# The low-half score pass of a head over 128 rows instead of 64, with zeros in a tile per head

## Chip, core and metric

The kernel runs on one core of a Trainium2 chip (trn2). The metric is the device time of one execution in microseconds (us); of several runs the median counts. Matrix products run on TensorE (PE; its weight loads stand in the trace as PEld), elementwise work on VectorE (DVE), ScalarE (ACT) and GpSimd (POOL), transfers are issued from the queue of SyncE (SP) or of POOL.

## What is computed

A sequence of 512 tokens with 1024 features goes through a block with three mixing branches and a feed-forward part, and then through two layers, each with eight heads of softmax attention ("fox" in the code), eight heads of retention ("ret") and a gated feed-forward part. The change touches the score products of three kinds of heads, 64 features wide: those of the first branch, of fox and of ret. Cut from the reference:

```
s = jnp.einsum('bqhd,bkhd->bhqk', q_blk, k_band).astype(jnp.float32) * scale + bias
...
logits = jnp.einsum('bhqd,bhkd->bhqk', qb, k).astype(jnp.float32) * scale
logits = logits + cq[..., :, None] - cum[..., None, :]
...
scores = jnp.einsum('bhid,bhjd->bhij', qc, kc) * intra_decay
```

## The kernel before

All activations lie feature-major: 128 features on the partitions, 512 tokens along the row. Every fp32 matrix is cut into two exact halves of the type fp32r (`xh`, `xl` of an activation, `wh`, `wl` of a weight), and a linear layer is three matmuls of 128x128 weights by 512 columns for each block of 128 features (`lin`, names `lin<-xh,wh`, `lin<-xh,wl`, `lin<-xl,wh`). These fill most of PE's time. The halves of the weights are made while the kernel runs, `wh` by ACT and `wl` by DVE.

Two heads of 64 features lie in one 128-row tile of q and one of k. `stack` (line 802) makes from such a pair: `ks`, a tile per head with the high half of k in the head's own 64 rows and the low half in the other 64; `qd`, a tile per head with the high half of q twice; and `ql`, one tile for both heads with the low half of q, each head in its own rows. A block of scores is then two products in one PSUM bank: `qd` with `ks` over 128 rows, and `ql` with `ks` over the head's 64 rows only:

```
return [[(qd[e], ks[e]), (ql[64 * e:64 * e + 64], ks[e][64 * e:64 * e + 64])] for e in range(2)], ...
```

`head` (line 825, first branch and fox) emits for each head four blocks of 128 queries with 128, 256, 384 and 512 keys; fox adds a third product with the constants `mkb` in bf16 that masks the diagonal block. `ret` (line 1713) emits four blocks of 128 keys with 512, 384, 256 and 128 queries. Every block is followed by DVE work that frees the PSUM bank (`lg<-sc,E`, or `st<-sc,dec`), then ACT, DVE and POOL, transposes (`pt`) and the products with the values (`po`).

The order is set when the program is recorded: every part is a coroutine, `Net.drive` (line 301) takes the ready one of the highest priority, and "ready" follows an estimated time of PE (`mm`, line 378) and of the queues of DVE, ACT and POOL (`Eng`, line 211). Each engine then runs its instructions in that fixed order. Tiles of 128x512 come from one pool of 66 (`g`), in the same order. DVE, ACT and POOL work is recorded by one helper (line 221), all matmuls by line 379, transposes by line 389.

Of the kernel before, what the change touches and what calls it, by code (L numbers as in the profile page):

```python
# [87 lines left out]
def _fm(w, kc=8):  # L88
    """[K, M] -> [M/128, K/(128*kc), 128, kc*128]: lhsT tiles, one column block at a time."""
    k, m = w.shape  # L90
    return np.ascontiguousarray(
        w.reshape(k // (128 * kc), kc, 128, m // 128, 128).transpose(3, 0, 2, 1, 4)
    ).reshape(m // 128, k // (128 * kc), 128, kc * 128)


def _tok(w):
    """[1024, 512] -> [4, 128, 2*512]: rhs rows, two row blocks per chunk."""
    return np.ascontiguousarray(w.reshape(4, 2, 128, 512).transpose(0, 2, 1, 3)).reshape(4, 128, 1024)


def _nar(w):
    """[1024, m] -> [128, 8*m]: lhsT rows of a narrow block."""
    return np.ascontiguousarray(w.reshape(KT, 128, -1).transpose(1, 0, 2)).reshape(128, -1)
# [98 lines left out]
class Ev:  # L202
    """a point in PE time, known once the work before it has been traced."""
# [7 lines left out]
class Eng:  # L211
    """an engine's instructions, with an estimate of when its queue is done."""
# [35 lines left out]
class Net:  # L248
# [39 lines left out]
    def w(self, *engs):  # L288
        """ns until the queues of these engines are done and seen to be."""
        return max(0.0, max(self.busy[e] for e in engs) - self.now) + self.LAT  # L290
# [4 lines left out]
    # ------------------------------------------------- cooperative emission  # L295
    # Each coroutine traces instructions and yields where a later one would wait:
    # None (go on at once), ns of PE time, an Ev, or a predicate.
# [46 lines left out]
    def take(self, role, n, cap):  # L344
        """wait for a place among the cap of a role."""
        while self.role.get(role, 0) + n > cap:
            yield lambda: self.role.get(role, 0) + n <= cap
        self.role[role] = self.role.get(role, 0) + n
# [43 lines left out]
    # ---------------------------------------------------------------- basics  # L392
# [32 lines left out]
    # ------------------------------------------------------ weights, linear  # L425
# [43 lines left out]
    def nextw(self):  # L469
        """the next chunk of weights as exact halves; the ones after it are set going."""  # L470
        i, n = self.wi, len(self.wq)
        if self.booting:
            self.wi += 1
            return self.wh.pop(i), self.wl.pop(i)
        self.fill()
        while self.wsh < min(n, i + 4):
            self.whi()
            while self.wsl < min(self.wsh - 1, i + 3):
                self.wlo()
        while self.wsl < min(n, i + 3, self.wsh):  # L480
            self.wlo()
        self.wi += 1
        return self.wh.pop(i), self.wl.pop(i)
# [19 lines left out]
    def lin(self, ps, w, off, xs, start=True, stop=True):  # L503
        """accumulate W^T x, each product of halves in its own pass."""
        wh, wl = w
        for k, x in enumerate(xs):
            yield from self.need(x)
            c = slice(off + 128 * k, off + 128 * k + 128)
            first, last = start and k == 0, stop and k == len(xs) - 1
            self.mm(ps, wh[:, c], x.h, first, False)  # L510
            self.mm(ps, wl[:, c], x.h, False, False)
            self.mm(ps, wh[:, c], x.l, False, last)
            yield None

    def proj(self, chunks, xs, evac):
        """task: one 128-row block of outputs; chunks: (dram, cols); xs: thunk."""
# [14 lines left out]
    def narrow(self, w, m, xs, evac):  # L531
        """task: a block of m outputs; the halves of its weights stand side by side, rows m to 2 m add to the first m."""
# [16 lines left out]
    def group(self, w, cut, xs, evacs):  # L549
        """task: several blocks at once, their last k tile after all the others; w: dram [blocks, 128, cols]."""  # L550
# [19 lines left out]
    def multi(self, chunk, parts):  # L570
        """task: one chunk that holds several blocks; parts: (offset, xs thunk, evac)."""
# [25 lines left out]
    def split(self, src, X_, free=True):  # L597
        """src -> hi, lo entries (coroutine)."""
# [10 lines left out]
    # ------------------------------------------------------------------ norm  # L609
    def feed(self, N, k, x, gain, done=None):  # L610
        """tile k of a norm's input: g x as halves, and its squares."""
# [34 lines left out]
    def rowsum(self, ps, a, n):  # L646
        """(coroutine) sums over each n rows of a feature-major tile, token-major: [128, S / n]."""
# [8 lines left out]
    def powm(self, src, n, scale, eps):  # L656
        """(coroutine) (scale src + eps)^-1/2."""
# [9 lines left out]
    def bcast(self, rt, n=NT):  # L667
        """(coroutine) token-major [128, NT] -> [128, S], the same on all partitions."""
# [11 lines left out]
    def rstd(self, N, n=D, eps=EPS):  # L680
        """(coroutine) 1/rms: N.rt token-major, N.rb broadcast."""
# [17 lines left out]
    # ------------------------------------------------------------- attention  # L699
    def values(self, chunks, nks, N, vs, centred=False):  # L700
        """task: token-major values, split: vs[t][e] = [keys, pair, (hi, lo) or (lo, hi), 64]."""
# [75 lines left out]
    def pv(self, h, vs, ph, pl, evs, y, yev):  # L777
        """(coroutine) y[rows of head h] = values^T p."""
# [23 lines left out]
    def stack(self, q, k):  # L802
        """(coroutine) a pair's q and k as exact halves, for two passes of products per head:
        [qh; qh] with [kh; kl], then ql with kh. Head 1 has its kh in the lower rows."""
        qh = yield from self.g("qh", F32R)
        self.ac.activation(qh, q.h, AF.Copy)
        qd, ks = [], []
        for e in range(2):
            r = slice(64 * e, 64 * e + 64)
            ks.append((yield from self.g("ks", F32R)))  # L810
            self.ac.activation(ks[e][r], k.h[r], AF.Copy)
        yield self.w("ac")
        ql = yield from self.g("ql", F32R)
# [6 lines left out]
        self.dv.tensor_tensor(out=ql, in0=q.h, in1=qh.bitcast(F32), op=ALU.subtract)  # L820
        self.free(qh, q.h, k.h)
        yield self.w("dv", "gp", "ac")
        return [[(qd[e], ks[e]), (ql[64 * e:64 * e + 64], ks[e][64 * e:64 * e + 64])] for e in range(2)], [[qd[0], ks[0]], [qd[1], ks[1], ql]]

    def head(self, h, qk, vs, y, yev, bias, mask, qdone, hdone):
        """(coroutine) softmax attention; q carries -scale, so scores come negated."""
# [70 lines left out]
    # --------------------------------------------------------------- block 1  # L897
# [73 lines left out]
    def load_x(self, N):  # L971
        """(coroutine) x and the first weights, in the order in which the first products take them."""
# [56 lines left out]
    def qk(self, w, N, out, c=None):  # L1029
        """task: projection to an fp32 tile (entry out)."""  # L1030
        self.proj([(w, 1024)], lambda: N.xs, self.qkev(N, out, c))
# [11 lines left out]
    def after(self, vs, n):  # L1043
        """count the heads that are done with vs."""
        vs.left -= n
        if vs.left == 0:
            self.vfree(vs)

    def heads(self, pr, q, k, vs, y, mk, mask, prio=2):
        """(coroutine) the two heads of a pair -> y entry. q, k: entries per head, rows of a head."""  # L1050
# [67 lines left out]
    def gates(self, n, upto, N):  # L1118
        """tasks: the gates of branch n below `upto` that are not yet there."""
# [61 lines left out]
    # ------------------------------------------------------------ HGRN branch  # L1181
    def logsig(self, z, f, s, out):
        """(coroutine) log sigmoid(z), with f = sigmoid(z) and s = sigmoid(-z); f is overwritten."""
# [10 lines left out]
    def gnorm(self, o, eps):  # L1194
        """(coroutine) per-head mean square of a pair tile -> 1/sqrt(ms + eps), broadcast in PSUM."""
# [24 lines left out]
    def silu(self, z):  # L1220
        """(coroutine) z <- z sigmoid(z)"""
# [7 lines left out]
    def blocks(self, t, off, stride, n, w):  # L1229
        """n blocks of w columns, `stride` apart, of a flat tile."""  # L1230
# [113 lines left out]
    def hlev(self, q, k, pre, suf, fifo):  # L1344
        """(coroutine) per level: q exp(sum since the block's middle), k exp(sum up to it)."""
# [35 lines left out]
    def near(self, t, n, dg):  # L1381
        """(coroutine) scores with at most one per key: the products t, at their keys, summed over each head."""
# [10 lines left out]
    def level(self, qt, kt, n, dg):  # L1393
        """(coroutine) scores of one level on the diagonal blocks, kept where they belong."""
# [54 lines left out]
    # ------------------------------------------------------------------- FFN  # L1449
    def xadd(self, m, ps, nxt=None):  # L1450
        """(coroutine) residual add of block m, then what follows it."""
# [46 lines left out]
    # --------------------------------------------------------------- block 2  # L1498
    def fin1(self, N1, N, m):
        """closing norm of block 1 folded with the opening norm of layer 0."""  # L1500
# [123 lines left out]
    def xout(self, m):  # L1624
        """block m of the residual stream to DRAM while attention needs the room."""
# [21 lines left out]
    def fgate(self, i, ps, N, cum):  # L1647
        """(coroutine) running sum of log sigmoid(f + bias), to DRAM for the broadcast loads."""
# [40 lines left out]
    def rotary(self, w, N, out, c, rot):  # L1689
        """task: projection with the rotary embedding."""  # L1690
# [85 lines left out]
    def ple_proj(self, i, half, out):  # L1776
        """tasks: half of p @ w_ple_proj, kept for the gate."""
# [132 lines left out]
    def last(self, chunks, N, pp, N4):  # L1910
        """task: the last two blocks of the gate in two halves of the tokens, each with its share of the closing norm."""
# [74 lines left out]
class BranchC:  # L1986
    """latent attention: shared preparation, then its pairs of heads."""
# [32 lines left out]
    def tables(self):  # L2020
        """cos and signed sin of position * frequency, 16 frequencies per 32 rows."""
# [143 lines left out]
class X:  # L2165
    """a tile (h), or its exact halves (h, l), ready at ev; s: the rows that count."""
# [40 lines left out]
```

## Time and profile before

| | |
|---|---|
| median of 3 runs | 2363.28 us (2362.02 to 2363.62) |
| profiled execution, first to last instruction | 2362.3 us |
| PE busy | 2326.2 us, 98% |
| DVE busy | 1509.7 us, 64% |
| ACT busy | 1070.2 us, 45% |
| POOL busy | 455.0 us, 19% |

The span of the profiled execution lies 1.0 us under the median of the runs. The recorded end of a matmul is modelled and overlaps the next one, so that PE counts as busy even where its matmuls start far apart; the distance from start to start is what a matmul costs.

### The profile page before, as it was taken

To read this page: it belongs to the slowest core of one execution; us is meant where nothing else is said; L and a number is where in the kernel's file an instruction comes from. 1 tells how busy PE (TensorE), PEld (TensorE's weight loads), DVE (VectorE), ACT (ScalarE), POOL (GpSimd) and SP (SyncE) were. 2 spreads that over 40 slices of the span, in tenths; PEclk is the share of its full clock that TensorE was granted. 3 is DMA by queue.
4 is the path that set the end of the run, shared out by engine and by line. 5 is a ranking of instruction groups with operands and counts; after the bars stand their busy time and mean duration, and the time that the engine had idled before them with its cause. 6 is when DMAs were issued, how large, how long until landed. Compare 5 with 4: busy or idle time off the path is not lost.

```text
span 2362.3 us, 28970 instructions
## 1 busy us (share of the span) xinstructions
PE 2326.2 (98%) x10810; PEld 1871.6 (79%) x10810; DVE 1509.7 (64%) x2355; ACT 1070.2 (45%) x1695; POOL 455.0 (19%) x531
## 2 busy tenths in 40 slices
PE   9999999999999999999999999999999999999998
PEld 7787877778888888777778888888777778888887
DVE  6778489976542554678866562457578866552466
ACT  5657466664321233555543331245555544331343
POOL 3423044431000002323330000002323320000012
PEclk9999999999999999999999999999999999999999
DMA  5222222223322332432332333333332332333332
GB/s 181 75 68 63 81 72 63 63 85 116 98 95 98 98 98 83 152 95 89 117 98 94 98 98 98 104 93 115 123 104 81 107 107 90 98 98 98 107 91 70
DMA packets 75725, 228.23 MB, mean 97 GB/s; under 512 B 9664, under 2 KB 15680, under 8 KB 75584
## 3 DMA queue, kind: packets, MB, share of 16 engines
q1 hardware_dynamic: 70400, 209.62, 28.2%
q0 software_dynamic: 5184, 16.75, 2.3%
q8 instruction: 85, 1.39, 0.3%
q14 instruction: 56, 0.46, 0.1%
HBM read 215.29 MB, written 6.32 MB: 94 GB/s over the span
## 4 chain that ended last, share of the span: by engine, by line
PE 91%; DVE 6%; issue 1%; ACT 1%; POOL 1%; DMA 0%; SPq 0%; POOLq 0%; DVEq 0%; ACTq 0%
PE lin L379 75%; PE v L379 6%; PE sc L379 5%; PE po L379 3%; PE pt L389 1%; DVE wl L221 1%; DVE dg L221 1%; DVE xl L221 1%; DVE eq L221 1%; DVE pre L221 0%; DVE suf L221 0%; DVE sl L221 0%; DVE gate L221 0%; ACT L221 0%; PE pb L389 0%
## 5 line engine op out<-in xcount | busy, mean ns | idle before, releaser
L379 PE MATMUL lin<-xh,wh 128*128 128x512 f32 (+1 forms) x2752 | 1095.9, 398 | 0.0
L379 PE MATMUL lin<-xl,wh 128*128 128x512 f32 (+1 forms) x2752 | 1072.4, 390 | 6.7 <-DVE xl L221 6.6
L379 PE MATMUL lin<-xh,wl 128*128 128x512 f32 (+1 forms) x2728 | 1061.8, 389 | 0.0
L221 DVE TENSOR_TENSOR wl<-raw,wh 128x1024 fp32r<-128x1024 f32 (+3 forms) x391 | 467.6, 1196 | 513.4 <-PE lin L379 335.7
L221 ACT ACTIVATE wh<-raw 128x1024 fp32r<-128x1024 f32 (+4 forms) x394 | 392.5, 996 | 821.7 <-PE lin L379 684.9
L379 PEld LDWEIGHTS lin<-xl,wh 128*128 128x128 f32 x2752 | 517.3, 188 | 117.7 <-DVE xl L221 8.8
L379 PEld LDWEIGHTS lin<-xh,wh 128*128 128x128 f32 x2752 | 517.4, 188 | 117.0 <-issue 11.7
L379 PEld LDWEIGHTS lin<-xh,wl 128*128 128x128 f32 x2728 | 514.2, 188 | 96.1
L221 POOL TENSOR_TENSOR sq<-sq 128x512 f32<-128x512 f32 (+1 forms) x61 | 90.6, 1485 | 571.5 <-ACT sq L221 570.8
L221 POOL TENSOR_SCALAR P<-P,r 128x128 f32<-128x128 f32 (+3 forms) x128 | 80.3, 633 | 198.7 <-DVE r L221 180.8
L221 POOL MEMSET pad<- 128x2 f32 x44 | 4.4, 100 | 586.7 <-DVE cv L221 586.7
L221 DVE SCALAR_TENSOR_TENSOR cv<-pad,vec,cv 128x512 f32<-128x512 f32 x88 | 66.1, 752 | 40.7 <-ACT cv L221 39.0
L221 DVE CUSTOM_DVE_ANT_0 lg<-sc,E 128x128 f32<-128x128 f32 (+1 forms) x96 | 46.6, 486 | 60.9 <-PE sc L379 53.7
L379 PE MATMUL v<-wh,xh 128*128 128x512 f32 x192 | 78.2, 407 | 2.3 <-POOL wh L221 2.3
L379 PE MATMUL v<-wl,xh 128*128 128x512 f32 x192 | 75.6, 394 | 1.5 <-DVE wl L221 1.4
L221 ACT ACTIVATE ph<-pt 128x512 fp32r<-128x512 f32 (+3 forms) x128 | 55.7, 435 | 45.5 <-PE pt L389 44.5
L379 PE MATMUL v<-wh,xl 128*128 128x512 f32 x192 | 75.5, 393 | 0.0
L221 ACT ACTIVATE P<-lg,m 128x128 f32<-128x128 f32 (+1 forms) x96 | 53.5, 558 | 39.7 <-DVE m L221 28.9
L221 DVE TENSOR_TENSOR x<-lin,x 128x512 f32<-128x512 f32 x80 | 54.6, 684 | 23.5 <-PE lin L379 23.4
L221 DVE TENSOR_TENSOR pl<-pt,ph 128x512 fp32r<-128x512 f32 (+3 forms) x128 | 60.4, 481 | 13.8 <-ACT ph L221 13.3
L221 ACT ACT_TABLE_LOAD x51 | 65.4, 1283 | 4.3 <-DVE qk L221 1.6
L221 ACT ACTIVATE tl<-po 64x512 f32<-64x512 f32 x56 | 33.2, 593 | 74.0 <-PE po L379 73.6
(243 smaller groups left out, 2558.6 us busy)
## 6 DMA issues: line engine op xcount, KB each, us to landing
raw<-wup SPq DMA_DIRECT2D x88, 512.0 KB, 3.3
raw<-w SPq DMA_DIRECT2D x83, 512.0 KB, 3.6
raw<-wf SPq DMA_DIRECT2D x64, 512.0 KB, 3.3
raw<-wdn SPq DMA_DIRECT2D x32, 512.0 KB, 3.5
raw<-wv SPq DMA_DIRECT2D x22, 512.0 KB, 3.6
raw<-wpg SPq DMA_DIRECT2D x16, 512.0 KB, 3.3
raw<-wbr SPq DMA_DIRECT2D x12, 512.0 KB, 3.3
raw<-wdn SPq DMA_DIRECT2D x16, 384.0 KB, 3.1
```

Of the source, the lines that this page charges most:

```text
L221: r = f(*a, **k)
L379: self.nc.tensor.matmul(out, l, r, start=start, stop=stop)
L389: self.nc.tensor.transpose(out, src, self.ident)
```

## The change

`stack` now makes a `ql` tile for each head: DVE writes the low half of q to the head's own 64 rows (two instructions of 64 rows in place of one of 128), POOL writes zeros to the other 64. The second product runs `ql` with the whole `ks` over 128 rows; the zeros take the low half of k out of the sum. A `ql` tile is freed with its own head. The rest of the diff takes out comments and docstrings and is not shown.

```diff
-        qd, ks = [], []
+        qd, ks, ql = [], [], []
         for e in range(2):
-            r = slice(64 * e, 64 * e + 64)
+            r, o = slice(64 * e, 64 * e + 64), slice(64 - 64 * e, 128 - 64 * e)
             ks.append((yield from self.g("ks", F32R)))
             self.ac.activation(ks[e][r], k.h[r], AF.Copy)
+            ql.append((yield from self.g("ql", F32R)))
+            self.pl.memset(ql[e][o].bitcast(F32), 0.0)
         yield self.w("ac")
-        ql = yield from self.g("ql", F32R)
         for e in range(2):
...
-        self.dv.tensor_tensor(out=ql, in0=q.h, in1=qh.bitcast(F32), op=ALU.subtract)
+        for e in range(2):
+            r = slice(64 * e, 64 * e + 64)
+            self.dv.tensor_tensor(out=ql[e][r], in0=q.h[r], in1=qh[r].bitcast(F32), op=ALU.subtract)
         self.free(qh, q.h, k.h)
         yield self.w("dv", "gp", "ac")
-        return [[(qd[e], ks[e]), (ql[64 * e:64 * e + 64], ks[e][64 * e:64 * e + 64])] for e in range(2)], [[qd[0], ks[0]], [qd[1], ks[1], ql]]
+        return [[(qd[e], ks[e]), (ql[e], ks[e])] for e in range(2)], [[qd[0], ks[0], ql[0]], [qd[1], ks[1], ql[1]]]
```

`stack` runs 20 times (4 pairs of the first branch, 4 of fox and 4 of ret in each of two layers).

On DVE this is the first `stack` of the program, as a piece of the difference:

```order
 L221 CAST lev<-lv 128x512
 L221 TENSOR_TENSOR ks<-qk,ks 64x512 x2
-L221 TENSOR_TENSOR ql<-qk,qh 128x512
+L221 TENSOR_TENSOR ql<-qk,qh 64x512 x2
 L221 TENSOR_TENSOR wl<-raw,wh 128x1024
 L221 SCALAR_TENSOR_TENSOR qk<-lin,rb 128x512
```

One instruction has become two at the same place, and the low half of a weight (`wl`) stands behind them.

On POOL this is the same place and the next pair, after the change (before, the two `MEMSET ql` rows are not there):

```order
L221 MEMSET ql 64x512 x2
L221 TENSOR_SCALAR qd<-qh 64x512 x2
L221 DMA E<-ext 128x512
L221 TENSOR_SCALAR E<-E 128x512
L221 MEMSET E 64x64
L221 DMA E<-ext 128x512
L221 MEMSET ql 64x512 x2
L221 TENSOR_SCALAR qd<-qh 64x512 x2
```

The zeros stand ahead of the copies of `qd` and of the load of a head's bias `E`.

The new estimates also shift the order a little. On PE, in the first layer, the second head of the third ret pair and the first head of the fourth stand together before the change:

```order
L379 MATMUL sc<-qd,ks 128x384
L379 MATMUL sc<-ql,ks 128x384
L379 MATMUL lin<-xh,wh 128x512
L379 MATMUL lin<-xh,wl 128x512
L379 MATMUL lin<-xl,wh 128x512
L379 MATMUL sc<-qd,ks 128x256
L379 MATMUL sc<-ql,ks 128x256
L379 MATMUL sc<-qd,ks 128x512
L379 MATMUL sc<-ql,ks 128x512
L379 MATMUL sc<-qd,ks 128x128
L379 MATMUL sc<-ql,ks 128x128
```

and after it the second head of the third pair stands alone, each block of scores followed by a linear step:

```order
L379 MATMUL sc<-qd,ks 128x384
L379 MATMUL sc<-ql,ks 128x384
L379 MATMUL lin<-xh,wh 128x512
L379 MATMUL lin<-xh,wl 128x512
L379 MATMUL lin<-xl,wh 128x512
L379 MATMUL sc<-qd,ks 128x256
L379 MATMUL sc<-ql,ks 128x256
L379 MATMUL lin<-xh,wh 128x512
L379 MATMUL lin<-xh,wl 128x512
L379 MATMUL lin<-xl,wh 128x512
L379 MATMUL sc<-qd,ks 128x128
L379 MATMUL sc<-ql,ks 128x128
```

The first head of the fourth pair has moved some 30 matmuls of linear layers down. Elsewhere the moves are of the same kind; the number of matmuls is unchanged.

## Rows read from the trace of the kernel before

**Rows 1.** The page, busy time: us busy, share of the span, instructions.

```profile
span 2362.3 us, 28970 instructions
...
PE 2326.2 (98%) x10810; PEld 1871.6 (79%) x10810; DVE 1509.7 (64%) x2355; ACT 1070.2 (45%) x1695; POOL 455.0 (19%) x531
```

**Rows 2.** All instructions on the tile ql: count, duration ns min/median/max, first and last start.

```profile
L379 PE MATMUL sc<-ks,ql x96: 322/410/503, 56.9 to 1828.6; 64*128 64x128 f32 x24, 64*128 64x256 f32 x24, 64*128 64x384 f32 x24, 64*128 64x512 f32 x24
...
L379 PE MATMUL sc<-ql,ks x64: 322/408/500, 1065.3 to 1883.7; 64*128 64x512 f32 x16, 64*128 64x384 f32 x16, 64*128 64x256 f32 x16, 64*128 64x128 f32 x16
L221 DVE TENSOR_TENSOR ql<-qk,qh x12: 691/692/1009, 48.8 to 1806.8; 128x512 fp32r<-128x512 f32 x12
```

**Rows 3.** Timeline, first head of the first branch: start us, duration us, engine, instruction.

```profile
56.73 0.22 PE L379 MATMUL sc<-ks,qd 128*128 128x128 f32 x1
...
57.47 0.40 PE L379 MATMUL lin<-xh,wl 128*128 128x512 f32 x1
...
57.94 0.28 PE L379 MATMUL sc<-ks,qd 128*128 128x256 f32 x1
...
58.80 0.39 PE L379 MATMUL lin<-xh,wl 128*128 128x512 f32 x1
...
60.48 0.39 PE L379 MATMUL lin<-xl,wh 128*128 128x512 f32 x1
...
60.70 0.40 PE L379 MATMUL sc<-ks,qd 128*128 128x512 f32 x1
...
61.03 0.18 PEld L379 LDWEIGHTS sc<-ks,ql 64*128 64x128 f32 x1 [0.36 <-issue]
61.03 0.50 PE L379 MATMUL sc<-ks,ql 64*128 64x512 f32 x1
...
61.46 0.50 PE L379 MATMUL lin<-xh,wh 128*128 128x512 f32 x1
...
61.80 0.40 PE L379 MATMUL lin<-xh,wl 128*128 128x512 f32 x1
```

**Rows 4.** Timeline of PE in the first layer: products with values, then a fox head.

```profile
1112.71 0.33 PE L379 MATMUL po<-pl,vs 128*128 128x384 f32 x1
1112.88 0.28 PE L379 MATMUL po<-ph,vs 128*128 128x256 f32 x1
1113.00 0.28 PE L379 MATMUL po<-pl,vs 128*128 128x256 f32 x1
...
1117.04 0.34 PE L379 MATMUL sc<-ks,qd 128*128 128x384 f32 x1
...
1117.68 0.23 PE L379 MATMUL sc<-mkb 128*128 128x128 bf16 x1
```

**Rows 5.** Timeline of the third branch: scores over 96 rows, then the mask.

```profile
177.89 0.38 PE L379 MATMUL sc<-q,q 96*128 96x128 f32 x2
...
178.11 0.22 PE L379 MATMUL sc<-mkb 128*128 128x128 bf16 x1
```

**Rows 6.** Busy time in stretches of the layers, all instructions: us, counts, then PE's granted clock.

```profile
1060.00:1170.00 110.00, 109.67 (x499) 80.30 (x499) 94.02 (x185) 66.72 (x132) 44.55 (x50) 1.00 0.30 89
1140.00:1170.00 30.00, 29.67 (x126) 21.29 (x125) 29.20 (x44) 19.91 (x35) 11.85 (x12) 1.00 0.28 82
```

**Rows 7.** The same stretches, instructions on ql alone: PE, PEld, DVE.

```profile
1060.00:1170.00 110.00, 17.67 (x43) 7.86 (x43) 4.15 (x6) 1.00 0.30 89
1140.00:1170.00 30.00, 4.59 (x11) 2.01 (x11) 1.38 (x2) 1.00 0.28 82
1840.00:1870.00 30.00, 4.58 (x11) 2.01 (x11) 1.39 (x2) 1.00 0.27 87
```

**Rows 8.** DVE on the tile ks, in the form of rows 2.

```profile
L221 DVE TENSOR_TENSOR ks<-ra,ks x16: 684/687/1815, 1061.5 to 1864.0; 64x512 fp32r<-64x512 f32 x16
```

**Rows 9.** POOL's groups: count, busy us, mean ns, idle before and its cause.

```profile
L221 POOL TENSOR_SCALAR qd<-qh 64x512 fp32r<-64x512 f32 x40 | 33.1, 828 | 34.7 <-ACT qh L221 33.0
...
L221 POOL MEMSET dg<- 128x512 f32 x8 | 3.9, 524 | 0.0
```

## Prediction

> **What bounds the kernel now.** I read the page first. PE is busy 98% of the span, DVE 64%, POOL 19% [rows 1], and in the stretches of the layers PE's clock is granted in full (1.00) [rows 6]: the time is what PE's matmuls cost, one after the other. PE's busy time can't tell what one costs, since ends are modelled; the distance from start to start in a timeline can. So I went to the timeline of the first head whose scores are made in the first branch, where all four widths come with linear steps between them.
>
> There the reader sees the normal step first: a linear matmul of 512 columns starts at 60.48 and the next matmul at 60.70, 0.22 us later (0.225 below; the same step is seen for whole linear layers). Then the pattern breaks [rows 3]. `qd` with `ks` starts at 60.70, `ql` with `ks` at 61.03 (0.33 instead of 0.225), the next linear matmul at 61.46 (0.43), and the one after it at 61.80 (0.34). The row of PEld at 61.03 gives the reason: the load of the weights for the 64-row product starts at the moment of its matmul, after 0.36 us in which no load ran, and nothing that the profile shows was waited for. The loads of the products over 128 rows run beside the matmul before. So a product over 64 rows between products over 128 costs 1.10 us for three matmuls that normally take 3 x 0.225 = 0.68: 0.42 us are lost.
>
> Is it the 64 rows, or just a score product? Scores of the third branch run over 96 rows, and there two passes of 128 columns and the start of the mask fit into 0.22 us (177.89 to 178.11), 0.11 each, with no gap [rows 5]. Products with the values over 128 rows follow each other at 0.17 (384 columns, 1112.71 to 1112.88) and 0.12 us (256 columns, 1112.88 to 1113.00) [rows 4]. Only the 64-row forms stand apart. There are 96 + 64 = 160 of them, a quarter at each width [rows 2].
>
> **What the change takes away.** After it both score products are 128-row products like their neighbours, so I price them at the normal steps: 0.225, 0.17, 0.12 and 0.11 us for 512, 384, 256 and 128 columns. The zeros add no columns. From the start of `qd` to the second linear matmul, [rows 3] have 1.10 us at 512 columns (normal 0.68), 0.86 at 256 (normal 0.12 + 0.12 + 0.225 = 0.465) and 0.74 at 128 (normal 0.445). Lost: 0.42, 0.395 and 0.295; 384 columns I put between the two widest, 0.40. The mean is 0.378. The first branch (32 products) and ret (64) are of this kind: 96 x 0.378 = 36.2 us.
>
> In fox the mask in bf16 follows `ql`. Up to its start [rows 4] show 1117.04 to 1117.68, 0.64 us at 384 columns, where 2 x 0.17 = 0.34 are normal: 0.30 lost. What comes behind the mask looks the same in the third branch, where no 64-row product precedes it, so I count nothing there. At the other widths I take the loss above without its last part (0.34 - 0.225 = 0.115): 0.305, 0.28 and 0.18. Mean 0.267, times 64 products: 17.1 us. Together PE has 53.3 us less to do, 0.33 a product.
>
> The Trainium skill (TensorEngine Tiling (Array Packing), Key Properties) says that a change of tiling mode, not of the tile alone, drains the engine. The gaps on both sides of each 64-row product agree with it, and by it the whole 53.3 us would go.
>
> **What it adds.** DVE: one more instruction in each of 20 `stack` calls. The old one over 128 rows took 0.69 us (up to 1.01) [rows 2]; one of the same kind over 64 rows, for `ks`, takes 0.69 as well [rows 8]. So 20 x 0.69 = 13.8 us. Behind it wait `wl` of the coming weights and the work on the scores. POOL: 40 memsets of 64x512; one of 128x512 takes 0.524 us [rows 9], so at most 21 us in all on an engine that is 81% idle. Two of them (1.05 us) stand ahead of the `qd` copies; those idle for ACT's `qh` before they start, 33.0 us over 40 [rows 9], so that about half of the memsets is covered. If this cover is gone, a `stack` comes 1.05 us later, at worst 21 us over all 20, if PE had nothing recorded between; it has linear layers there. One more tile of 128x512 is held per pair: no cost of its own, it shifts the recorded order.
>
> **How much of the 53.3 us arrives.** PE gets ahead only where the others keep up. In 1060 to 1170 of the first layer DVE is busy 94.0 of 110 us, and in its last 30 us 29.2 of 30 [rows 6]. 43 of the layer's 64 products lie in the longer stretch, 11 in the last 30 us, and again 11 in the twin of these in the second layer [rows 7]. Where DVE has no idle time PE can't gain: 22 x 0.33 = 7.3 us don't come. Of the new DVE work, 6 of each layer's `stack` calls fall into the longer stretch (6 old `ql` instructions there, [rows 7]); I charge these in full, 12 x 0.69 = 8.3 us, and hide the rest behind DVE's idle time elsewhere. The bounds of this term are 0 (everything hidden) and 13.8 to 20.2 us (all 20 at 0.69 or 1.01). The order helps a little: the two ret heads that stand together before the change, at the end of the full stretch, stand apart after it; I give it nothing.
>
> Sum: -53.3 + 7.3 + 8.3 = -37.7 us. Against the profiled execution's 2362.3 this is 2324.6; its span lies 1.0 under the median of the runs, so I predict **2325.5 us**.
>
> **The rivals.**
>
> *DVE becomes the bound of the layers.* After the change the stretch of 110 us would hold 110 - 43 x 0.33 = 95.7 us of PE and 94.0 + 6 x 0.69 = 98.1 us of DVE. DVE was packed to 97% in the last 30 us and to 85% over all 110 [rows 6]. At 97% the stretch takes 101.1 us, a gain of 8.9 instead of 14.3; at 93%, 105.5; at 88%, 111.5, a loss of 1.5. In the last case the change gives 53.3 - 2 x 15.8 = 21.7 us: 2341.6. For it speaks that DVE, ACT and PE hand each other the tiles of a head in turn; against it that weight halves are made chunks ahead, so that DVE may lag for a while. Chance 0.20.
>
> *Nothing goes.* The gap could belong to the `ql` product itself, to its operands or to the order in which PE's loads are issued, and stay with 128 rows. Then PE gains nothing and the layers pay the 8.3 us of DVE at most: 2363.3 to 2371.6. The Trainium skill (TensorE: Matmul & The Clock Gate, Part 3: Packing small matmuls) states that a weight load overlaps matmuls in flight only when its row group differs, which speaks against whole-array products: by it the loads of the new passes would lie bare too. Against this the trace has the steps of 0.225 us in which loads over 128 rows run beside matmuls over the same 128 rows [rows 3]; the 96-row scores say the same [rows 5]. Chance 0.07.
>
> *Slower: a memset holds POOL's queue.* A `ql` tile is taken from the pool of 66 earlier than before, and its memset waits for the last reader of the buffer. POOL is in order: behind it stand `qd`, the load of `E` and the scaling of the probabilities, for which PE waits. If each of the 20 calls held PE for 3 us, this would cost 60 us against 53.3 and, with the 8.3 us of DVE, end at 2363.3 + 15 = 2378. It decides from (53.3 - 8.3) / 20 = 2.25 us a call on. Against it stands POOL's idle time, and that a buffer comes back only once the program's estimate has its reader done. Chance 0.06.
>
> *All of it arrives*, 2310 or less, if DVE's new work hides and the full stretches loosen: the lower end of the main case and a little beyond, 0.05 beyond.
>
> **How the numbers follow.** The main case has the remaining 0.62; its own range goes from 2310.0 (nothing charged) to 2337.5 (all of 20.2 us of DVE, and 7.3 that don't come). The range for 8 in 10 reaches into the rival in which DVE bounds the layers and leaves out the two in which nothing is gained: **2307 to 2347 us**. A difference of 0.2% (4.7 us) is about what a measurement here can tell from none. Faster by more: main, DVE and full arrival, 0.62 + 0.20 + 0.05 = 0.87. Within 0.2%: most of the case in which nothing goes, 0.05. Slower: the rest of it and the held queue, 0.08.
>
> **What would show it.** In the changed trace every second score product should read 128x128, its weight load should run beside the matmul before, and `qd`, `ql` and two linear matmuls of 512 columns should start 0.22 to 0.23 us apart. The stretch of each layer's heads should be 14 to 20 us shorter, the first branch about 12, nothing else. DVE should have 20 more instructions and be full for longer near the end of the layers' heads, with some waits of PE for `pl` or `ql` there. I am wrong in the step on the 64 rows if the gap of 0.33 to 0.43 us is still there with 128; wrong in the step on DVE if PE's waits on DVE stay near zero or eat more than 16 us; wrong on POOL if PE or ACT wait for a memset.

## The result and the profile after

The changed kernel takes 2324.09 us (median of 4 runs, 2323.04 to 2325.01), the kernel before 2363.45 us (median of 4 runs, 2362.02 to 2365.72). The ratio is 0.9832, 95% interval 0.9818 to 0.9846: 39.4 us or 1.7% faster. 2325.5 was predicted, with 2307 to 2347 as its range.

The page of the changed kernel, from its first line, its busy times (as in [rows 1]) and its chain of work that ended last:

```profile
span 2323.2 us, 29048 instructions
...
PE 2278.9 (98%) x10810; PEld 1868.2 (80%) x10810; DVE 1518.4 (65%) x2375; ACT 1067.4 (46%) x1695; POOL 479.0 (21%) x571
...
PE 87%; DVE 8%; issue 2%; POOL 1%; ACT 1%; DMA 0%; SPq 0%; POOLq 0%; DVEq 0%; ACTq 0%
```

The kernel is still bound by PE, which issues as many matmuls as before. DVE has its 20 instructions more, POOL its 40. In the chain PE's share is 87% where it was 91%, and DVE's 8% where it was 6%.

Instructions on the tile `ql`, as in [rows 2]:

```profile
L379 PEld LDWEIGHTS sc<-ks,ql x96: 187/188/192, 58.7 to 1793.5; 128*128 128x128 f32 x96
L379 PE MATMUL sc<-ks,ql x96: 273/308/397, 58.8 to 1793.7; 128*128 128x128 f32 x24, 128*128 128x256 f32 x24, 128*128 128x384 f32 x24, 128*128 128x512 f32 x24
...
L221 POOL MEMSET ql<- x40: 517/520/526, 35.1 to 1823.2; 64x512 f32 x40
L221 DVE TENSOR_TENSOR ql<-qk,qh x24: 682/689/1011, 50.1 to 1777.7; 64x512 fp32r<-64x512 f32 x24
L221 DVE TENSOR_TENSOR ql<-ra,qh x16: 682/687/990, 1049.3 to 1832.7; 64x512 fp32r<-64x512 f32 x16
```

The product now reads 128 rows and its recorded time has fallen from 410 ns (median) to 308. The new DVE instructions take the 0.69 us that were charged, a memset of 64 rows takes 0.52.

The timeline of the first heads of the first branch, to be held against [rows 3] (some rows of other engines and of PEld are left out):

```profile
59.64 0.28 PE L379 MATMUL sc<-ks,qd 128*128 128x256 f32 x1
59.75 0.28 PE L379 MATMUL sc<-ks,ql 128*128 128x256 f32 x1
59.87 0.40 PE L379 MATMUL lin<-xh,wh 128*128 128x512 f32 x1
60.10 0.40 PE L379 MATMUL lin<-xh,wl 128*128 128x512 f32 x1
...
61.62 0.39 PE L379 MATMUL sc<-ks,qd 128*128 128x512 f32 x1
61.62 0.19 PEld L379 LDWEIGHTS sc<-ks,ql 128*128 128x128 f32 x1
61.84 0.39 PE L379 MATMUL sc<-ks,ql 128*128 128x512 f32 x1
61.84 0.19 PEld L379 LDWEIGHTS lin<-xh,wh 128*128 128x128 f32 x1
62.07 0.40 PE L379 MATMUL lin<-xh,wh 128*128 128x512 f32 x1
62.31 0.39 PE L379 MATMUL lin<-xh,wl 128*128 128x512 f32 x1
```

At 512 columns the way from `qd` to the second linear matmul is 62.31 - 61.62 = 0.69 us; it was 1.10. At 256 columns it is 0.46, where it was 0.86. The weight load of `ql` now starts at 61.62, together with the matmul before its own.

A fox head of the first layer, to be held against [rows 4]:

```profile
1060.95 0.34 PE L379 MATMUL sc<-ks,qd 128*128 128x384 f32 x1
1061.13 0.34 PE L379 MATMUL sc<-ks,ql 128*128 128x384 f32 x1
1061.31 0.23 PE L379 MATMUL sc<-mkb 128*128 128x128 bf16 x1
```

From `qd` to the mask it is 0.36 us; it was 0.64.

The loss at all 160 products can be added up: for each the steps from start to start of the matmul before it, of its own and of the one behind, less the normal step of their width (0.227, 0.174, 0.119 and 0.110 us for 512, 384, 256 and 128 columns). That makes 51.4 us before (13.0 in the first branch, 38.4 in the two layers) and 1.4 us after; these 1.4 are two waits for `pl`, 0.7 us each, that fall among the steps counted. So PE has 50.0 us less to do, and 39.4 arrive. A good part of the rest shows as waits that are new or longer. The view of PE's waits of the changed kernel has among others, by cause (us in total, times, longest):

```profile
PE pt L389 <- POOL P L221: 3.9, 6, 1.3
PE po L379 <- DVE pl L221: 2.4, 4, 0.7
```

Before, PE never waited for `P`, and for `pl` once, 0.2 us. Waits for `wl` and `eq` also grew, by 1.7 and 1.1 us, and one for `wh` shrank by 1.6. Windows of the stretch of the layers' heads, the first layer and then the second (length, then busy us of PE, PEld, DVE, ACT, POOL, PE's granted clock, and at the end the DMA's share and GB/s):

```profile
1040.00:1150.00 110.00, 106.42 (x543) 87.23 (x543) 100.77 (x197) 68.36 (x134) 56.74 (x67) 1.00 0.32 99
1730.00:1840.00 110.00, 106.21 (x538) 87.19 (x537) 99.83 (x201) 69.08 (x137) 52.63 (x61) 0.98 0.32 101
```

DVE is busy for 100.8 of 110 us there; in the like stretch before it was 94.0 [rows 6]. The timeline shows how a wait for `P` comes about (first layer; rows of several views, the others left out; an entry in brackets is the idle time before the instruction and what ended it):

```profile
1065.98 0.15 DVE L221 RECIPROCAL r<-sum 128x1 f32<-128x1 f32 x1
1066.16 4.64 POOL L221 TENSOR_SCALAR P<-P,r 128x256 f32<-128x256 f32 x1
1066.37 0.68 DVE L221 TENSOR_TENSOR rb<-rb,rot 128x512 f32<-128x512 f32 x1
1066.97 0.15 DVE L221 RECIPROCAL r<-sum 128x1 f32<-128x1 f32 x1
...
1068.43 0.54 DVE L221 TENSOR_TENSOR pl<-st,ph 128x384 fp32r<-128x384 f32 x1
1068.90 1.21 DVE L221 TENSOR_TENSOR wl<-raw,wh 128x1024 fp32r<-128x1024 f32 x1
1070.04 0.41 DVE L221 TENSOR_TENSOR pl<-st,ph 128x256 fp32r<-128x256 f32 x1
...
1070.85 0.33 PE L389 MATMUL pt<-cst,P 128*128 128x128 f32 x1 [1.33 <-POOL P L221]
1071.44 0.33 PE L389 MATMUL pt<-cst,P 128*128 128x128 f32 x1 [0.26 <-POOL P L221]
1072.14 0.33 PE L389 MATMUL pt<-cst,P 128*128 128x128 f32 x1 [0.37 <-POOL P L221]
```

POOL scales the probabilities `P` by reciprocals `r`, which DVE makes. The reciprocals are not late: the last of this head's is done at 1067.12. It is POOL's own instruction that is long: one on a `P` of 128x256 lasts 4.64 us, where the median of its shape is 0.48 and the longest before the change was 1.83. All that time DVE runs without a gap (rotary products, `st`, `pl`, halves of weights), and POOL's instruction ends 0.35 us after a subtraction for `pl`. PE's transposes wait behind it. The second layer has the same, 4.64 us from 1751.19. That DVE's work holds POOL's instruction is inferred from these times; rot_out, below, bears on it.

In the second layer the clock falls behind this wait (a window as above):

```profile
1757.00:1760.40 3.40, 3.23 (x10) 2.78 (x11) 0.76 (x2) 1.18 (x3) 2.22 (x5) 0.50 0.77 264
```

PE has waited for `P` for 1.30 and 0.26 us, and from 1757.0 on its clock is granted at half (0.50), that is 1.2 GHz, for 3.4 us; the matmuls that start there take some 1.5 us more than their normal steps. This is where the 0.98 above comes from. The kernel before has no such stretch between 1243 and 1939. What is left of the 10.6 us that did not arrive is not assigned to causes here.

### The profile page after: what moved, and what is told of

Its sections match the earlier page's. It is cut to its first block, busy times and chain, and to the rows that moved or that the text cites. A ratio compares the mean times of both kernels' runs of the same rounds, so it can differ in the third digit from the quotient of the medians.

```text
span 2323.2 us, 29048 instructions
## 1 busy us (share of the span) xinstructions
PE 2278.9 (98%) x10810; PEld 1868.2 (80%) x10810; DVE 1518.4 (65%) x2375; ACT 1067.4 (46%) x1695; POOL 479.0 (21%) x571
## 4 chain that ended last, share of the span: by engine, by line
PE 87%; DVE 8%; issue 2%; POOL 1%; ACT 1%; DMA 0%; SPq 0%; POOLq 0%; DVEq 0%; ACTq 0%
PE lin L379 73%; PE v L379 5%; PE sc L379 3%; PE po L379 3%; DVE wl L221 2%; PE pt L389 2%; DVE xl L221 1%; DVE dg L221 1%; DVE eq L221 0%; DVE ks L221 0%; DVE pre L221 0%; DVE qk L221 0%; DVE ql L221 0%; DVE sl L221 0%; DVE suf L221 0%
## 5 line engine op out<-in xcount | busy, mean ns | idle before, releaser
L221 POOL TENSOR_SCALAR P<-P,r 128x128 f32<-128x128 f32 (+3 forms) x128 | 86.5, 681 | 149.3 <-DVE r L221 133.0
```

Source lines behind the costliest of these rows:

```text
L221: r = f(*a, **k)
```

## The experiments

Each run is compared with runs of the kernel before on the same chip. The median of before was 2364.09 us for the first four, 2362.96 for the next four and 2363.46 for the last two.

### Only the rows: shared128

The kernel before, with the old shared tile, its order and its DVE work; only the second product runs over all 128 rows.

```diff
-        return [[(qd[e], ks[e]), (ql[64 * e:64 * e + 64], ks[e][64 * e:64 * e + 64])] for e in range(2)], [[qd[0], ks[0]], [qd[1], ks[1], ql]]
+        return [[(qd[e], ks[e]), (ql, ks[e])] for e in range(2)], [[qd[0], ks[0]], [qd[1], ks[1], ql]]
```

> The kernel before with one edit: the second score product takes the old shared ql tile and the whole ks over 128 rows. No zeros, no second tile, no added DVE or POOL work, the recorded order of before. (The sum then also holds the other head's low half of q times this head's low half of k, which the reference doesn't have.) Theory of the rows: the gaps around 160 products go, 52 to 53 us, of which some 7 don't arrive where DVE is full: 2317 us (2311 to 2322), faster than the change, which pays for its added DVE work. Rival, the added work is hidden and only the full stretches count: 2324, as the change. Rival, the gain came from the new order or the separate tiles: 2350 or more.

Measured: 2320.76 us, ratio 0.9819 (0.9804 to 0.9834). The rows alone bring 43.3 us. By the same sum of starts the loss at the products is 1.6 us here, so 49.8 us left PE and 6.5 did not arrive, with no work added.

### All but the rows: rows64_new

The changed kernel, with its tiles, zeros, DVE work and order, and the product over 64 rows again.

```diff
-        return [[(qd[e], ks[e]), (ql[e], ks[e])] for e in range(2)], ...
+        return [[(qd[e], ks[e]), (ql[e][64 * e:64 * e + 64], ks[e][64 * e:64 * e + 64])] for e in range(2)], ...
```

> The changed kernel with everything that it adds (zeros, tile per head, two DVE instructions, its order), but the second product again over the head's own 64 rows. Theory of the rows: the gaps are back and the added work stays: 2363 to 2376 us. Rival, the order or the tiles gave the gain: 2324 to 2335.

Measured: 2364.19 us, ratio 1.0001 (0.9991 to 1.0011); the loss at the products is 51.3 us again. The whole gain hangs on the rows. And with the gaps in place the added work and the new order together cost nothing, as would be if DVE did that work while PE stands in them. Another reading is that the new order paid for the work here too; no run has the gaps and the work in the old order.

### The product or the switch: low_twice

The kernel before, with each 64-row product issued twice in a row (here for `head`; `ret` likewise).

```diff
             for j, (q, k) in enumerate(qk):
+                if j == 1:
+                    self.nc.tensor.matmul(ps[:, :w], q[:, 128 * i:w], k[:, :w], start=False, stop=False)
                 self.mm(ps[:, :w], q[:, 128 * i:w], k[:, :w], j == 0, mask is None and j == len(qk) - 1)
```

> The kernel before, with the second score product over 64 rows issued twice in a row, so that the low half of q counts twice. If the gap belongs to going from 128 to 64 rows and back, the copy costs a normal step of its width, 0.156 us on average: 160 x 0.156 = 25, 2383 to 2393 us, and start to start 0.11 to 0.23 us between the two copies. If each 64-row product pays the gap by itself: 0.156 + 0.2 to 0.33 us each, 2420 to 2441.

Measured: 2390.18 us, ratio 1.0111 (1.0096 to 1.0126), 26.1 us more, or 0.163 us for each of the 160 copies; the mean normal step of the four widths is 0.157. The sum of losses stays at 51.6 us with twice as many 64-row products. The timeline at 512 columns, where the first copy stands at line 837 (rows of PE and PEld, some of PEld left out):

```profile
62.06 0.40 PE L379 MATMUL sc<-ks,qd 128*128 128x512 f32 x1
62.39 0.18 PEld L837 LDWEIGHTS sc<-ks,ql 64*128 64x128 f32 x1 [0.36 <-issue]
62.39 0.50 PE L837 MATMUL sc<-ks,ql 64*128 64x512 f32 x1
62.50 0.19 PEld L379 LDWEIGHTS sc<-ks,ql 64*128 64x128 f32 x1
62.73 0.39 PE L379 MATMUL sc<-ks,ql 64*128 64x512 f32 x1
63.05 0.19 PEld L379 LDWEIGHTS lin<-xh,wh 128*128 128x128 f32 x1 [0.36 <-issue]
63.05 0.50 PE L379 MATMUL lin<-xh,wh 128*128 128x512 f32 x1
63.38 0.40 PE L379 MATMUL lin<-xh,wl 128*128 128x512 f32 x1
```

The load of the second copy starts at 62.50, beside the first one's matmul: a 64-row load behind a 64-row product is not held. The loads at 62.39 and 63.05, where 64 follows 128 and 128 follows 64, are. So the cost belongs to the change between the two, in both directions, and not to a product over 64 rows. From the first `qd` to the second linear matmul it is 1.32 us for four matmuls that normally take 0.90: 0.42 lost, as with one copy. One sign that was expected did not come: from copy to copy it is not the normal step but 0.16, 0.22, 0.28 and 0.34 us (medians at 128 to 512 columns), 0.05 to 0.11 more. By as much the step behind the second copy is shorter than that behind the only one before (0.32 instead of 0.43 at 512 columns), so that the loss is spread otherwise and its sum stays.

### The order of before: order_before

The changed kernel with the memset and one of the two DVE instructions issued outside the program's estimates, so that the recorded order is that of before but for these instructions.

```diff
-            self.pl.memset(ql[e][o].bitcast(F32), 0.0)
+            self.nc.gpsimd.memset(ql[e][o].bitcast(F32), 0.0)
...
-            self.dv.tensor_tensor(out=ql[e][r], in0=q.h[r], in1=qh[r].bitcast(F32), op=ALU.subtract)
+            dv = self.nc.vector if e else self.dv
+            dv.tensor_tensor(out=ql[e][r], in0=q.h[r], in1=qh[r].bitcast(F32), op=ALU.subtract)
```

> The changed kernel, with the added DVE and POOL instructions kept out of the estimates that set the order, so that the order of before is kept but for a few steps. Theory (the order matters little): 2320 to 2328 us. Rival, the two ret heads that the new order sets apart were worth something: 2330 to 2340. Rival, the new order lost time: 2312 to 2318.

Measured: 2330.94 us, ratio 0.9861 (0.9846 to 0.9875). Against the changed kernel's 2324.09 the new order is worth 6.9 us (the two intervals only touch, at 0.9846), which no step of the prediction had; against shared128, which has the same order, it is 10.2 us longer with the added work (how much of this is the work, see below). Here PE waits for `pl` seven times, 3.7 us, and for `P` five times, 2.4 us.

### More DVE work: dve_more

The changed kernel, both `ql` instructions of every `stack` issued twice, in the same order: 40 more.

```diff
+        for e in (0, 1):
+            r = slice(64 * e, 64 * e + 64)
+            self.nc.vector.tensor_tensor(out=ql[e][r], in0=q.h[r], in1=qh[r].bitcast(F32), op=ALU.subtract)
         self.free(qh, q.h, k.h)
```

> The changed kernel in its own order, each of the 40 low-half instructions of DVE issued a second time right behind (the same values are written again): 27.6 us more DVE work in the stretches of the heads. Theory that DVE is on the path there, as charged (12 of 20 instructions in full): about 60% arrives, +14 to +20 us, 2338 to 2344. If added DVE work of this kind is hidden: 2324 to 2327.

Measured: 2349.16 us, ratio 0.9938 (0.9924 to 0.9952). 27.6 us of DVE work cost 25.1 us, more than was expected. PE's waits in this run:

```profile
PE po L379 <- DVE pl L221: 9.8, 10, 1.5
...
PE pt L389 <- POOL P L221: 5.9, 7, 2.1
...
PE pt L389 <- DVE pl L221: 3.8, 2, 1.9
PE sc L379 <- DVE ql L826: 3.2, 4, 1.2
```

The two waits of the changed kernel have grown from 6.3 to 15.7 us, and two more stand beside them. Once the gaps are gone, DVE work added in the heads' stretch lies almost wholly on the path. Some 3 us of the 25.1 come by way of the clock: behind waits of 2.1 us for `P` and 1.9 us for `pl` in the first layer stand two stretches at 1.2 GHz that the changed kernel doesn't have:

```profile
1076.90:1080.30 3.40, 3.25 (x10) 2.79 (x11) 0.77 (x2) 1.20 (x3) 2.21 (x5) 0.50 0.76 249
1104.20:1107.60 3.40, 3.40 (x12) 2.84 (x11) 3.40 (x7) 0.85 (x2) 0.00 (x0) 0.50 0.26 52
```

### More zeros: pool_more

The changed kernel, every memset issued twice, in the same order.

```diff
             self.pl.memset(ql[e][o].bitcast(F32), 0.0)
+            self.nc.gpsimd.memset(ql[e][o].bitcast(F32), 0.0)
```

> The changed kernel in its own order, each of the 40 memsets of zeros issued twice on POOL: 20.8 us more POOL work. Theory that the zeros are covered by POOL's idle time: 2323 to 2326 us. If the zeros hold POOL's queue (the rival on the slow side, in small): 2330 or more, with waits of PE on POOL's scaling of P.

Measured: 2323.36 us, ratio 0.9834 (0.982 to 0.9848): no difference, with 20.8 us of memsets more on POOL. The zeros are hidden, with as much room again.

### The new order without the added work: shared_neworder

The changed kernel's estimates kept (POOL's and DVE's clocks are moved on by what the left-out instructions would have taken), so that its order stays, with one shared `ql` tile, one DVE instruction, no memsets, and the product over 128 rows.

```diff
-            self.pl.memset(ql[e][o].bitcast(F32), 0.0)
+            self.busy["gp"] = max(self.busy["gp"], self.now) + 595.0
...
-        for e in range(2):
-            r = slice(64 * e, 64 * e + 64)
-            self.dv.tensor_tensor(out=ql[e][r], in0=q.h[r], in1=qh[r].bitcast(F32), op=ALU.subtract)
+        self.dv.tensor_tensor(out=ql[1], in0=q.h, in1=qh.bitcast(F32), op=ALU.subtract)
+        self.busy["dv"] += 608.5
...
-        return [[(qd[e], ks[e]), (ql[e], ks[e])] for e in range(2)], ...
+        return [[(qd[e], ks[e]), (ql[1], ks[e])] for e in range(2)], ...
```

> The changed kernel's order and its 128-row products, but with one shared ql tile again: one DVE instruction, no zeros (the same extra low-low sum as in shared128); the estimates that set the order are kept. If the added work costs what shared128 and order_before differ by (10 us) in either order: 2312 to 2317 us, the fastest so far. If the new order had hidden the added work: 2321 to 2325.

Measured: 2316.36 us, ratio 0.98 (0.9787 to 0.9814), the lowest of all. In the new order the kernel with the added work is 2324.09 - 2316.36 = 7.7 us longer. The order without the work is worth 4.4 us against shared128, at the edge of what can be told (the two intervals overlap from 0.9804 to 0.9814).

### Relief for DVE: rot_pool, rot_out and ql_pool

Three ways to take about 11 to 14 us from DVE. The first moves one of two rotary products of each `ret` tensor to POOL, 16 instructions; estimates and order are kept.

```diff
-            self.dv.tensor_tensor(out=b, in0=b, in1=rot.h[1], op=ALU.mult)
+            nc.gpsimd.tensor_tensor(out=b, in0=b, in1=rot.h[1], op=ALU.mult)
+            self.busy["dv"] = max(self.busy["dv"], self.now) + 608.5
```

> The changed kernel in its own order, with one of the two rotary products of ret moved from DVE to POOL (16 instructions, 0.69 us of DVE each, 11 us less DVE work in the layers, some 22 us more on POOL). If a full DVE keeps 10 us of the gain from arriving: 3 to 7 us of it come, 2317 to 2321. If the loss is elsewhere, or POOL becomes the wait: 2324 or more.

Measured: 2324.39 us, ratio 0.9836 (0.9822 to 0.985): nothing gained. On POOL the product takes 1.59 us, and PE's wait for POOL's `P` is 4.4 us instead of 3.9, that for `pl` 1.9 instead of 2.4. That left open whether DVE is the limit at all, or whether POOL took back what DVE gave. The next run takes the same product away and gives POOL nothing.

```diff
-            self.dv.tensor_tensor(out=b, in0=b, in1=rot.h[1], op=ALU.mult)
+            self.busy["dv"] = max(self.busy["dv"], self.now) + 608.5
```

> The changed kernel without one of the two rotary products of a ret pair of q or k (the product with the sine table, 16 instructions of DVE, 128x512, 0.68 us each, 10.9 us in all); the sum behind it takes the unrotated values, so that retention is computed with other q and k. The recorded order is that of the changed kernel. POOL gets nothing in return, unlike in the run that moved this product there. If a full DVE in the stretch of the layers' heads is what holds PE back, the time falls by 6 to 11 us, to 2313 to 2318, as 27.6 us of DVE work more cost 25.1. Rival: the last microseconds hang on single short waits (POOL's P behind the reciprocals, pl) that this work, which lies ahead of the heads, does not set; then 2320 to 2325.

Measured: 2318.59 us, ratio 0.9808 (0.9793 to 0.9823), 5.5 us under the changed kernel for 10.9 us of DVE work, between the two theories and nearer to the first. The interval just overlaps that of the changed kernel (0.9818 to 0.9823), so the 5.5 us are at the edge of what can be told. PE's two waits halve:

```profile
PE pt L389 <- POOL P L221: 1.9, 5, 0.5
PE po L379 <- DVE pl L221: 1.2, 2, 0.6
```

The wait that the profile puts down to POOL's `P` shrinks with DVE work alone: POOL's long instruction on `P`, during which the product that is left out used to run, lasts 3.60 us instead of 4.64, in both layers, and the stretch at 1.2 GHz behind it in the second layer is gone. With dve_more, where more DVE work costs 25.1 us clear of the intervals, this says that DVE does hold PE back. Moved to POOL, the product gains nothing: POOL seems to take back what DVE gave. The last run tries the same with the added work itself: the second `ql` of each `stack` on POOL.

```diff
+            if e:
+                nc = self.nc
+                nc.gpsimd.tensor_tensor(out=ql[e][r], in0=q.h[r], in1=qh[r].bitcast(F32), op=ALU.subtract)
+                self.busy["dv"] = max(self.busy["dv"], self.now) + 608.5
+            else:
+                self.dv.tensor_tensor(out=ql[e][r], in0=q.h[r], in1=qh[r].bitcast(F32), op=ALU.subtract)
```

> The changed kernel with the second of the two low halves of q of each stack made on POOL instead of DVE, same recorded order and same numbers: DVE loses 20 instructions of 0.69 us, POOL gets 20, of some 0.8 to 1.5 us each (its 64-row copies take 0.83, its two-operand products of 128x512 1.5). Theory: the added DVE work costs 7.7 us, and most of it comes back, 2317 to 2321, faster than the changed kernel. Rival: POOL's own queue holds P or qd behind it, as in the run that moved a rotary product to POOL: 2322 to 2328.

Measured: 2324.81 us, ratio 0.9832 (0.9816 to 0.9848): no gain. The subtractions that make `ql` in the first branch and in fox in this run:

```profile
L825 POOL TENSOR_TENSOR ql<-qk,qh x12: 1286/1726/1778, 47.9 to 1777.3; 64x512 fp32r<-64x512 f32 x12
L221 DVE TENSOR_TENSOR ql<-qk,qh x12: 682/872/1687, 48.5 to 1775.9; 64x512 fp32r<-64x512 f32 x12
```

On POOL one takes 1.73 us instead of 0.69 on DVE, and the DVE instruction that runs beside it has a median of 0.87 and a longest time of 1.69 (in ret 1.73 on POOL, and 0.68 and 1.00 on DVE). POOL stays no place for this work.

## Why the prediction was right

Its steps, with what they measured:

| step | predicted, us | measured, us | from |
|---|---|---|---|
| gaps at 160 products go | -53.3 | -50.0 | sum of starts, before and after |
| of it the first branch | -12.1 | -12.0 | the same, 13.0 to 1.0 |
| does not arrive where DVE is full | +7.3 | +6.5 | shared128 |
| added DVE work (with the zeros) | +8.3 | +10.2 in the old order, +7.7 in the new | order_before less shared128; after less shared_neworder |
| of it in the layers' heads | +8.3 | +8.4 and +5.0 | the same pairs, matmul by matmul in the profiled executions |
| zeros on POOL | 0 | 0 | pool_more |
| recorded order | 0 | -6.9 | after less order_before |

Along one path the kernels give -49.8 + 6.5 + 10.2 - 6.9 = -40.0 us, which is 2324.09 less the 2364.09 of before that the first four experiments were compared with. These are differences of the same medians, so they must add up; it is no further test.

**The 64 rows.** The step that carried the forecast held: the gap belongs to the change between products over 64 and over 128 rows. The rows of the profile had shown it on both sides of each product, and low_twice shows that it is paid for each change and not for each product. The sum was 3.3 us too high. By kind, as the loss before less that after, the first branch gave 12.0 us (12.1 predicted), fox 17.0 (17.1) and ret 21.0 (24.2): the estimate of fox held, and ret fell short, 1.4 us of it by the two waits for `pl`. The Trainium skill (TensorEngine Tiling (Array Packing), Key Properties) says that changing the mode drains the engine, and low_twice agrees, with the same loss for one product and for two. The rule that was set against it (the Trainium skill, TensorE: Matmul & The Clock Gate, Part 3: Packing small matmuls), by which a load overlaps only when its row group differs, does not agree when it is read alone, as the prediction read it; the same section also names the background weight buffer as a case in which a load is pulled ahead. Here the load of `ql` over 128 rows starts at 61.62, with the matmul over the same 128 rows before it.

**DVE.** Its charge had about the right size. The medians differ by 10.2 us in the old order and by 7.7 in the new, but not all of this is the added work. The two kernels of each pair have the same order on PE, so that a matmul of the one can be set against the matmul of the same number in the other. From shared128 to order_before the delay grows by 3.9 us in the first layer's heads and by 4.5 in the second's, 8.4 of 12.1 us in all; from shared_neworder to the changed kernel by 2.9 and 2.1, 5.0 of 8.9. Part of the rest arises where none of the added work is: 1.8 and 1.4 us in the first 30 us, ahead of the first `stack`, and in the second pair 3.1 us between 1890 and 1930, behind the last. At these places the slower execution has stretches granted at 1.2 GHz (3.4 us from 22.7 and from 23.0, 6.8 us from 1900.3) that the faster one lacks. rows64_new, with the same instructions as the changed kernel in its first 30 us, lacks the first too, so that it looks like chance; one profile of each kernel can't settle it.

Hiding the work of the remaining `stack` calls was too kind as a rule: of dve_more's delay against the changed kernel, which has the same order, 22.9 us arise in the layers' heads (some 3 of them by way of the clock), where its added work is 32 x 0.69 = 22.1 us. The rival in which DVE becomes the bound gave 2341.6; the kernel stayed 17.5 us below it, and dve_more, with three times the added work, lies above it. PE did wait for `pl`, as was written; it waited longer for `P`, which had not been named, and rot_out shows that this depends on DVE's work too, by way of a POOL instruction that lasts longer while DVE is full.

**The zeros.** They cost nothing, as was said, but the reason given was misread: POOL's 33.0 us of idle time ahead of the `qd` copies [rows 9] are not spread over the 40 copies; they stand in front of 5 of the 20 pairs (12.6, 4.1, 6.3, 5.0 and 5.0 us). pool_more shows that the room is there all the same.

**The full stretches.** 6.5 us did not arrive in the old order and 51.9 - 46.6 = 5.3 in the new (the loss at the products and the time of shared_neworder, against before): near 7.3. That half of a relief of DVE came back in rot_out speaks for the place; that DVE had no idle time there is argued from its windows, and no run separates it from single late tiles.

**The order.** This step failed in size: the prediction saw that two `ret` heads move apart, and gave it nothing. By the medians it was worth 6.9 us with the added work, where the two intervals only touch, and 4.4 without it, where they overlap: its sign is likely, its size not settled. That the sum still came within 1.5 us is partly luck: PE had 3.3 us less to gain than thought, and a term put at nothing paid for it. Which of the moves brought it was not tried.

**By stage.** Linear matmuls with the same number start 12.0 us earlier after the change at 130 us of the run before, behind the first branch (about 12 were predicted). By 990 us, ahead of the layers, 9.3 of this are left, though nothing was predicted for the stages between. The first layer gains 15.8 more and the second 13.6, where 14 to 20 were predicted: the second is a little short.

## What to carry to other kernels

Judge a small matmul among large ones by the distance from start to start of it and of both neighbours: one over fewer rows can cost more than a whole one padded with zeros, as 0.42 us a product did here, because the engine pays for going there and back (products over 96 rows showed no such gap at 128 columns, [rows 5]); where it can't be padded, put such products next to each other. When such gaps go, price added work on the engine that is next in line nearly in full, and look for it also behind waits that carry another engine's name: an instruction there may last longer than its kind. Set two kernels of the same order against each other matmul by matmul before a difference of a few microseconds is put down to the edit: part of it may lie where the edit does nothing. A diff that changes a scheduler's estimates also changes its order: run the new work in the old order and the old work in the new one before crediting the edit.

## What was not expected of the hardware

A memset over 64 rows takes 0.520 us, one over 128 rows of the same 512 columns 0.524 [rows 9], and a DVE subtraction 0.689 against 0.692 [rows 2]: half the rows save nothing there. A matmul behind another over 64 rows has the recorded time of a 128-row one (302 ns against 308, medians), while the first in line has 410. And the same 64x512 subtraction takes 1.73 us on POOL, two and a half times its time on DVE. A POOL instruction of 0.48 us lasted 4.64 while DVE ran without a gap, and a wait of PE of little more than a microsecond was followed by 3.4 us at half the clock, which cost some 1.5 us more.
